# Softmax rows divided inside the transposing matmuls by a diagonal of reciprocals, and one adaLN chunk finished before the recurrence

## The chip, the cores and the metric

One core of one Trainium2 chip runs the whole step as a single program. The metric is the device time in microseconds (us) of one execution; less is better. The engines named below are PE (matmuls; its weight loads are listed as PEld), DVE (VectorE), ACT (ScalarE), POOL (GpSimd) and SP (SyncE, which issues most transfers).

## The reference, cut to what matters

One trunk layer over 1024 latent and 256 context tokens, model width 1024, in float32. The parts that the change touches are the attention and the adaLN modulation:

```python
def adaln(cond, w_ada, b_ada):
    m = jax.nn.silu(cond.astype(F32)) @ w_ada.astype(F32) + b_ada.astype(F32)
    return jnp.split(m[..., None, :], N_MOD, axis=-1)      # N_MOD = 6

def one_block(qi):                                          # per 128 queries
    s = jnp.einsum('bqkgd,bskd->bkgqs', qi, kf) * scale
    p = jax.nn.softmax(s, axis=-1)
    return jnp.einsum('bkgqs,bskd->bqkgd', p, vf)
```

There are 8 query heads of 64 channels over 2 key/value heads. Latent queries attend to 512 cached and 1024 latent keys; context queries attend to the 256 context keys. Beside the attention there is a gated linear recurrence (HGRN2, 4 heads, two directions), and after both come the output projections and a squared-ReLU MLP.

## The kernel before, in words

All matmuls of the projections and of the MLP are done as three float32r products of split operands (a high part `hi` and a low part `lo`, names `hs`, `wsp`, `ah`, `wh`), so PE is used three times for each weight tile (lines 319 to 321 and 336 to 338). Instructions on PE stand in the order in which the program is written; the other engines are ordered by a scheduler, which takes priorities (`tc.high_priority`) and explicit successions (`tc.issue_after`).

The attention is cut into units of one head and 256 queries (two blocks `j` of 128): 32 latent units with keys in three tiles of 512 (index `i`), and 8 context units with one tile of 256. For each block and key tile, `score` makes 128 x 512 scores (L819), DVE takes row maxima (L820), `expo` writes `pexp` on ACT with the row sums beside it (L830), DVE adds and inverts the sums into `rs` (L833, L834), and `norm` multiplies each tile of `pexp` in place by `rs` (L838), alternately on POOL and on DVE. Then `trans` transposes four 128 x 128 pieces of `pexp` into one PSUM tile `ps_t` by four PE instructions whose moving operand is the identity (L860); ACT and DVE split that tile into `pTh` and `pTl` (L863), and `value` multiplies the two by the values (L874, L875). A latent unit has six such steps, a context unit one, so there are 32 * 6 + 8 = 200 groups of four transposes. A list of events with fixed offsets orders these steps on PE, and between them a filler `fz` puts matmuls of other input projections and of the adaLN weights.

adaLN's weights come in 16 chunks of 256 columns. `ada_cols` multiplies a chunk (L176) into a PSUM tile of tag `g` (three buffers, shared with the projections' outputs), copies it out on ACT (`ev`, L178), and returns `late`, which transposes it into the same PSUM tile (L182), reduces it on DVE (`adas`, L185) and adds the bias (`modc`, L186). The `late` parts wait in the list `todo`, and are taken out during a later projection group.

After the attention, `hgrn` runs 24 recurrence units (head, direction, token tile), filled up with the gate projections. `prep` of a unit makes its decays and keys with scans and products on DVE, ACT and POOL (L1008 to L1044), `keys_t` transposes its keys `uf` on PE (L1072), `scores`, `states_` and `out` do the matmuls (L1083, L1095, L1114, L1116). `prep` of the next unit is placed behind the last copy of keys and the last product that made keys. The tile `R` that the scans read is set by POOL (L1244, L1245).

Of the kernel before, what the change touches and what calls it, by code (L numbers as in the profile page):

```python
# [12 lines left out]
ALU = mybir.AluOpType  # L13
AX = mybir.AxisListType

P = 128
# [28 lines left out]
def build(ctx, tc, I, O, C):  # L45
    nc = tc.nc
    v, s_, g_, pe, sp = nc.vector, nc.scalar, nc.gpsimd, nc.tensor, nc.sync
# [8 lines left out]
    def pool(name, side="left"):  # L56

        st = open_pools[name] = ExitStack()
        return st.enter_context(tc.tile_pool(name=name, bufs=1, side=side, reuse_waits="tile"))
# [13 lines left out]
    def PS(tag, shape=(P, 512)):  # L73
        tag = "g" if tag == "p" else tag
        return ps.tile(list(shape), F32, tag=tag, name="ps_" + tag, bufs=PSB[tag])

    def S(shape=(P, 512), dt=F32, name=None, ring=None):
        ring = ring or RING_OF[name]
        return (xb if ring == "X" else sb if ring in "DE" else sl).tile(list(shape), dt, tag="s" + ring, name=name, bufs=RINGS[ring])
# [14 lines left out]
    def T(n, name="tiny"):  # L94
        return tp.tile([P, n], F32, tag="tiny%d" % n, name=name, bufs=8 if n <= 16 else 2)
# [7 lines left out]
    def store(out, in_):  # L103
        g_.dma_start(out=f32(out), in_=f32(in_))

    def f32(ap):
        return ap.bitcast(F32)


    ident0 = S((P, P), name="ident0")  # L110
# [3 lines left out]
    ident = f32(ident_r)  # L114
# [53 lines left out]
    ones = cp.tile([P, 1], F32, name="ones")  # L168
    v.memset(ones, 1.0)

    def ada_cols(pa, raw, ci):

        for k in range(4):
            for q in range(4):
                kq = 4 * (q // 2) + k
                pe.matmul(pa[32 * q:32 * q + 32, 0:P], ada_l[:, kq, :], raw[:, kq, (q % 2) * P:(q % 2 + 1) * P], start=(k == 0), stop=(k == 3))  # L176
        ev = S((P, P), name="ev")
        s_.activation(ev, pa[:, 0:P], AF.Copy)  # L178

        def late():  # L180
            pt = pa[:, P:2 * P]
            pe.transpose(pt, ev, ident)  # L182
            x = T(4, "adas")
            with tc.high_priority(offset=600):
                v.tensor_reduce(x.rearrange("p (c r) -> p c r", c=2), pt.rearrange("p (i c x) -> p c x i", i=2, c=2)[:, :, 0:2, :], axis=AX.X, op=ALU.add)  # L185
            v.tensor_tensor(modc[:, :, ci:ci + 2], x.rearrange("p (c r) -> p r c", c=2),  # L186
                            cols[:, B_ADA + ci:B_ADA + ci + 2].unsqueeze(1).broadcast_to([P, 2, 2]), op=ALU.add)
        return late
# [240 lines left out]
    KG = [512, 512, 512, 256]  # L429
# [244 lines left out]
    for idx in range(len(steps)):  # L674
        if idx > KC:
            ahead(idx + AHEAD + (idx > 11) + (idx > 13))
        t, kc = steps[idx]
# [105 lines left out]
    class Unit:  # L783
# [24 lines left out]
        def score(self, j, i):  # L808
            nk = len(self.kts)
            if (j, i) == (0, 0):  # L810
                self.qh = q_at[self.h, self.t]
                self.ps, self.mx, self.sm, self.rs = {}, {}, {}, {}
            if i == 0:
                self.mx[j], self.sm[j] = T(4, "mx"), T(4, "sm")
            n = KG[self.kts[i]]
            q0 = self.q2 * 256 + j * P
            pq = PS("s")
            for var in range(2):
                pe.matmul(pq[:, 0:n], self.qh[:, q0:q0 + P], K[self.g][var][self.kts[i]], start=(var == 0), stop=(var == 1))  # L819
            v.tensor_reduce(self.mx[j][:, i:i + 1], pq[:, 0:n], axis=AX.X, op=ALU.max)  # L820
            self.ps[j, i] = pq
            if i == nk - 1:
                ngm = T(1, "ngm")
                v.tensor_reduce(ngm, self.mx[j][:, 0:nk], axis=AX.X, op=ALU.max, negate=True)  # L824
                self.mx[j] = ngm
# [7 lines left out]
                v.tensor_reduce(rs, self.sm[j][:, 0:nk], axis=AX.X, op=ALU.add)  # L833
                v.reciprocal(rs, rs)  # L834

        def norm(self, j, i):
            x = self.Ps[j][i][:, 0:KG[self.kts[i]]]
            NORM[(i + j) % len(NORM)].tensor_scalar(x, x, self.rs[j], None, op0=ALU.mult)  # L838

        def events(self, s0):  # L840
            if self.nstep == 1:
                ev = [(-4, 0, 0), (-3.5, 1, 0)]
                out = [(a, self.score, (j, i)) for a, j, i in ev]
                out += [(a + 1, self.expo, (j, i)) for a, j, i in ev]
                out += [(a + 2, self.norm, (j, i)) for a, j, i in ev]
            else:
                out = [(a, self.score, (j, i)) for (j, i), a in zip(self.tasks, (-7, -6.9, -6, -4, -3.9, -3))]
                out += [(a, self.expo, (j, i)) for (j, i), a in zip(self.tasks, (-5.4, -4.9, -4.4, -2.4, -1.9, -1.4))]
                out += [(a, self.norm, (j, i)) for (j, i), a in zip(self.tasks, (-4.35, -3.45, -2.45, -1.35, 0.1, 2.1))]
            for p2 in range(self.nstep):  # L850
                out.append((p2, self.trans, (p2,)))
                out.append((p2 + ((2.5, 2.3, 2.0, 1.7, 1.5, 1.3)[p2] if self.nstep > 1 else 1.5), self.value, (p2,)))
            return [(s0 + a, f, x) for a, f, x in out]

        def trans(self, p2):
            pt = PS("t", (P, 2, 256))
            for a in range(2):
                i, kg, b = self.kt[2 * p2 + a]
                for j in range(2):
                    pe.transpose(pt[:, a, j * P:(j + 1) * P], self.Ps[j][i][:, b * P:(b + 1) * P], ident)  # L860
            hi = S((P, 2, 256), F32R, name="pTh")
            lo = S((P, 2, 256), F32R, name="pTl")
            behind[:] = s_.activation(hi, pt, AF.Copy), v.tensor_tensor(lo, pt, f32(hi), op=ALU.subtract)  # L863
            self.pt[p2] = hi, lo
# [21 lines left out]
            if self.h % 2 == 1 and self.q2 == n // 256 - 1:  # L886
                dma(OA[self.h // 2][self.t], o_at[self.h // 2, self.t][:, 0:n])

    NORM = [g_, v]
    gone, keyed, copied = [None], [None], [None]  # L890
    q_at, o_at = {}, {}
    K = [[[None] * 4 for _ in range(2)] for _ in range(2)]
# [256 lines left out]
    def hgrn(fill, before):  # L1149

        units = [HUnit(6 * h + j, h, d, t) for h in range(4) for j, (d, t) in enumerate(((0, 0), (0, 1), (1, 1), (1, 0), (0, 2), (1, 2)))]
        fwd = {u.h: {} for u in units}
        for u in units:
            u.fwd = fwd[u.h].get(u.t)
            fwd[u.h][u.t] = u
        N, LATE = len(units), 3

        share = [u.n + 128.0 for u in units] + [300.0] * LATE
        tot, done, st = sum(share), 0.0, None
        with tc.issue_after(gone[0].ins):  # L1160
            units[0].prep()
        before()
        units[0].keys_t()
        for i in range(N + LATE):
            part = lambda x: fill.to((done + x * share[i]) / tot)
            if i + 1 < N:
                with ExitStack() as after:
                    after.enter_context(tc.issue_after(copied[0].ins))
                    after.enter_context(tc.issue_after(keyed[0].ins))
                    units[i + 1].prep()  # L1170
            if i < N:
                u = units[i]
                part(0.25)
                u.scores(u.fwd)
                part(0.5)
                u.states_(u.st or st)
                st = u.last
                if u.t == 2:
                    store(O["new_state_hgrn"][u.d, u.h], st)
                part(0.75)  # L1180
            if i >= LATE and units[i - LATE].d == 1:
                units[i - LATE].out_t()
            if 1 <= i <= N:
                units[i - 1].out(units[i - 1].fwd)
            part(0.95)
            if i + 1 < N:
                units[i + 1].keys_t()
            if 1 <= i <= N and units[i - 1].d == 1:
                units[i - 1].gate(units[i + 1] if i + 1 < N else None)
            part(1.0)  # L1190
            done += share[i]
# [17 lines left out]
    todo = []  # L1209
# [67 lines left out]
    for t in MT:  # L1277
        n = TT[t][1]
        for c in range(8):
            r = S(name="or")  # L1280
# [18 lines left out]
    for c2 in range(4):  # L1299
        r = wp.tile([P, 8, 256], F32, tag="wraw", name="wraw", bufs=2)  # L1300
        for i, nm in enumerate(("w_hgrn_out", "w_attn_out")):
            dma(r[:, 4 * i:4 * i + 4, :], I[nm][:, c2 * 256:(c2 + 1) * 256].rearrange("(k p) c -> p k c", p=P))
        for half in range(2):
# [4 lines left out]
            for t in MT:  # L1308
                n = TT[t][1]
# [108 lines left out]
    for b, half in turns:  # L1418
        t, off = b // 4, (b % 4) * P
# [62 lines left out]
    def raw1(i):  # L1482
        return wraw(I["w_ff1"], KC, i * 256)
# [30 lines left out]
    for i in range(NP):  # L1514
        r = raw1(i)
        for half in range(2):
            j = 2 * i + half
# [5 lines left out]
            if half == 0:  # L1523

                x = pw.tile([P, 4, P], F32, tag="at", name="at", bufs=4)
# [43 lines left out]
    ev = pool("ev", "right")  # L1569
    W2 = I["w_ff2"]  # L1570
    op0 = []
# [303 lines left out]
    x = fw_tile("y34")  # L1875
# [85 lines left out]
```

## Time and profile before

| | |
|---|---|
| time, median of 3 runs | 2056.77 us (2056.67 to 2057.38) |
| the profiled execution's own time | 2056.44 us |
| its span in the trace | 2054.7 us |
| granted TensorE clock, mean | 0.998 |
| PE busy | 2013.7 us (98%) |
| PE weight loads busy | 1735.2 us (84%) |
| DVE / ACT / POOL busy | 1407.0 / 941.1 / 533.1 us |

The span lies 1.7 us under the execution's time. "Busy" of PE is the union of its instructions' durations. A matmul's duration reaches past the start of the next one, so for PE the distance from start to start says what an instruction takes up; the timeline gives starts. A row of groups reads: line, engine, operation, output<-inputs, shapes, count, then busy time, mean duration of one, and the engine's idle time before them with what ended it. A row of the timeline reads: start, length, engine, line, operation, and in brackets the idle time before it; several like instructions are merged with their count.

### The profile page before, as it was taken

To read this page: it belongs to the slowest core of one execution; us is meant where nothing else is said; L and a number is where in the kernel's file an instruction comes from. 1 tells how busy PE (TensorE), PEld (TensorE's weight loads), DVE (VectorE), ACT (ScalarE), POOL (GpSimd) and SP (SyncE) were. 2 spreads that over 40 slices of the span, in tenths; PEclk is the share of its full clock that TensorE was granted. 3 is DMA by queue.
4 is the path that set the end of the run, shared out by engine and by line. 5 is a ranking of instruction groups with operands and counts; after the bars stand their busy time and mean duration, and the time that the engine had idled before them with its cause. 6 is when DMAs were issued, how large, how long until landed. Compare 5 with 4: busy or idle time off the path is not lost.

```text
span 2054.7 us, 33792 instructions
## 1 busy us (share of the span) xinstructions
PE 2013.7 (98%) x12470; PEld 1735.2 (84%) x12470; DVE 1407.0 (68%) x2733; ACT 941.1 (46%) x1973; POOL 533.1 (26%) x526
## 2 busy tenths in 40 slices
PE   7899999999999999999999999999999999999998
PEld 5698889988889978888888889988888888888886
DVE  5866776767776788879254635886666666577686
ACT  4634555555555423333321335755455544333443
POOL 1452233333333355545112101222122110000120
PEclk9999999999999999999999999999999999999999
DMA  9452220321212454554644533854444489455764
GB/s 318 160 189 78 70 83 32 104 88 55 77 50 80 132 176 158 165 168 158 199 136 149 179 113 119 253 184 152 159 146 157 145 292 361 147 160 175 232 238 142
DMA packets 220612, 317.38 MB, mean 154 GB/s; under 512 B 18760, under 2 KB 139808, under 8 KB 220448
## 3 DMA queue, kind: packets, MB, share of 16 engines
q1 hardware_dynamic: 207968, 275.32, 41.8%
q0 software_dynamic: 12480, 39.91, 5.2%
q8 instruction: 98, 1.61, 0.3%
q14 instruction: 66, 0.54, 0.1%
HBM read 229.43 MB, written 85.74 MB: 153 GB/s over the span
## 4 chain that ended last, share of the span: by engine, by line
PE 87%; DVE 6%; DMA 3%; ACT 2%; issue 1%; SPq 0%; POOL 0%; POOLq 0%; DVEq 0%; ACTq 0%
PE ps_g L319 8%; PE ps_g L321 7%; PE ps_g L320 7%; PE ps_s L819 4%; PE ps_t L860 4%; PE ps_g L1749 2%; PE ps_g L1748 2%; PE ps_g L1750 2%; PE ps_s L1593 2%; PE ps_s L1594 2%; PE ps_s L1595 2%; PE ps_g L875 2%; PE ps_s L1748 2%; PE ps_s L1749 2%; PE ps_s L1750 2%; PE ps_g L336 2%
## 5 line engine op out<-in xcount | busy, mean ns | idle before, releaser
L319 PE MATMUL ps_g<-hs,wsp 128*128 128x512 f32 (+1 forms) x896 | 322.5, 360 | 4.0 <-DVE adas L185 4.0
L321 PE MATMUL ps_g<-hs,wsp 128*128 128x512 f32 (+1 forms) x896 | 309.6, 345 | 0.0
L320 PE MATMUL ps_g<-hs,wsp 128*128 128x512 f32 (+1 forms) x896 | 309.3, 345 | 0.0
L838 POOL TENSOR_SCALAR pexp<-pexp,rs 128x512 f32<-128x512 f32 (+1 forms) x104 | 169.4, 1635 | 367.0 <-ACT pTh L863 174.4
L286 ACT ACTIVATE wsp<-wraw 128x512 fp32r<-128x512 f32 (+1 forms) x186 | 116.7, 667 | 228.6 <-PE ps_g L320 90.8
L287 DVE TENSOR_TENSOR wsp<-wraw,wsp 128x512 fp32r<-128x512 f32 (+1 forms) x186 | 147.0, 812 | 98.2 <-ACT wsp L286 97.7
L319 PEld LDWEIGHTS ps_g<-hs,wsp 128*128 128x128 f32 x896 | 169.9, 190 | 24.9 <-issue 4.6
L321 PEld LDWEIGHTS ps_g<-hs,wsp 128*128 128x128 f32 x896 | 169.5, 189 | 21.6
L863 ACT ACTIVATE pTh<-ps_t 128x512 fp32r<-128x512 f32 x200 | 118.6, 603 | 143.8 <-PE ps_t L860 142.4
L320 PEld LDWEIGHTS ps_g<-hs,wsp 128*128 128x128 f32 x896 | 170.2, 190 | 15.0
L286 ACT ACTIVATE ah<-ar 128x640 fp32r<-128x640 f32 (+1 forms) x112 | 80.9, 723 | 186.5 <-PE ps_g L1749 102.3
L820 DVE TENSOR_REDUCE mx<-ps_s 128x1 f32<-128x512 f32 (+1 forms) x208 | 137.2, 663 | 41.6 <-PE ps_s L819 40.7
L830 ACT ACTIVATE pexp<-ps_s,ngm 128x512 f32<-128x512 f32 (+1 forms) x208 | 137.5, 670 | 36.0 <-DVE ngm L824 35.2
L863 DVE TENSOR_TENSOR pTl<-ps_t,pTh 128x512 fp32r<-128x512 f32 x200 | 135.4, 680 | 18.0 <-ACT pTh L863 17.8
L287 DVE TENSOR_TENSOR ah<-ar,ah 128x640 fp32r<-128x640 f32 (+1 forms) x112 | 91.9, 821 | 77.0 <-ACT ah L286 75.8
L819 PE MATMUL ps_s<-Kl,Ql 128*128 128x512 f32 (+1 forms) x416 | 131.0, 412 | 1.0 <-ACT pexp L830 0.9
L860 PE MATMUL ps_t<-ident,pexp 128*128 128x128 f32 x800 | 121.4, 273 | 4.3 <-DVE pexp L838 3.0
L336 PE MATMUL ps_g<-wsp,hs 128*128 128x256 f32 x400 | 115.9, 290 | 0.0
L338 PE MATMUL ps_g<-wsp,hs 128*128 128x256 f32 x400 | 112.9, 282 | 0.0
L337 PE MATMUL ps_g<-wsp,hs 128*128 128x256 f32 x400 | 112.6, 281 | 0.0
L875 PE MATMUL ps_g<-pTl,Vl 128*128 128x256 f32 x400 | 105.4, 286 | 3.6 <-DVE pTl L863 3.5
L860 PEld LDWEIGHTS ps_t<-ident,pexp 128*128 128x128 f32 x800 | 93.7, 140 | 16.2 <-DVE pexp L838 4.6
(422 smaller groups left out, 5379.1 us busy)
## 6 DMA issues: line engine op xcount, KB each, us to landing
ar<-AF SPq DMA_DIRECT2D x112, 320.0 KB, 3.3
wraw<-in_w_ff SPq DMA_DIRECT2D x32, 1024.0 KB, 6.2
wr<-in_w_ff SPq DMA_DIRECT2D x128, 256.0 KB, 4.3
wraw<-in_w_in SPq DMA_DIRECT2D x18, 1024.0 KB, 5.6
wraw<-in_w_ada SPq DMA_DIRECT2D x16, 1024.0 KB, 5.7
AF<-a POOLq DMA_DIRECT2D x48, 256.0 KB, 2.8
AF<-t POOLq DMA_DIRECT2D x48, 256.0 KB, 2.3
wa<-in_w_ada SPq DMA_DIRECT2D x32, 256.0 KB, 6.0
```

Source lines behind the costliest of these rows:

```text
L286: s_.activation(hi, raw, AF.Copy)
L287: return v.tensor_tensor(lo, raw, f32(hi), op=ALU.subtract)
L319: pe.matmul(out, hi[:, k, :], mh, start=(first and k == 0), stop=False)
L320: pe.matmul(out, hi[:, k, :], ml, start=False, stop=False)
L321: pe.matmul(out, lo[:, k, :], mh, start=False, stop=(last and k == kcs - 1))
L336: pe.matmul(po[:, bb, :], mh[:, off:off + P], wh[:, k % 4, :], start=(k == 0), stop=False)
L819: pe.matmul(pq[:, 0:n], self.qh[:, q0:q0 + P], K[self.g][var][self.kts[i]], start=(var == 0), stop=(var == 1))
L830: s_.activation(e[:, 0:n], self.ps.pop((j, i))[:, 0:n], AF.Exp, bias=self.mx[j], accum_out=self.sm[j][:, i:i + 1])
L838: NORM[(i + j) % len(NORM)].tensor_scalar(x, x, self.rs[j], None, op0=ALU.mult)
L860: pe.transpose(pt[:, a, j * P:(j + 1) * P], self.Ps[j][i][:, b * P:(b + 1) * P], ident)
L863: behind[:] = s_.activation(hi, pt, AF.Copy), v.tensor_tensor(lo, pt, f32(hi), op=ALU.subtract)
L875: pe.matmul(pv[:, 0:256], V[self.g][kg][:, b, :], lo[:, a, :], start=False, stop=(k == last))
```

## The change

Three things are edited.

1. `norm` and its 208 instructions go. In their place `diag` writes, once for each block of 128 queries, the identity scaled by `rs` into one of four slots of a new tile `dg` (80 DVE instructions of 128 x 128). `trans` multiplies `pexp` (stationary) by that slot (moving) with an ordinary matmul, in the place of the transposes against the identity.
2. `dg` lies in the same one-buffer ring `K` as `ident0` before it and `R` after it.
3. The last chunk's `late` part is called ahead of the recurrence's loop, behind the first unit's `keys_t`, and the second unit's `prep` is placed behind that chunk's reduction `adas`.

```diff
@@ ada_cols.late
-                v.tensor_reduce(x..., pt..., axis=AX.X, op=ALU.add)
+                adas[0] = v.tensor_reduce(x..., pt..., axis=AX.X, op=ALU.add)
@@ Unit
-        def norm(self, j, i):
-            x = self.Ps[j][i][:, 0:KG[self.kts[i]]]
-            NORM[(i + j) % len(NORM)].tensor_scalar(x, x, self.rs[j], None, op0=ALU.mult)
+        def diag(self, j):
+
+            DG["n"] += 1
+            self.dg[j] = DG["t"][:, DG["n"] % 4]
+            v.tensor_scalar(self.dg[j], ident, self.rs[j], None, op0=ALU.mult)
...
-                out += [(a, self.norm, (j, i)) for (j, i), a in zip(self.tasks, (-4.35, -3.45, -2.45, -1.35, 0.1, 2.1))]
+                out += [(a, self.diag, (j,)) for j, a in ((0, -4.35), (1, -1.35))]
...
-                    pe.transpose(pt[:, a, j * P:(j + 1) * P], self.Ps[j][i][:, b * P:(b + 1) * P], ident)
+                    pe.matmul(pt[:, a, j * P:(j + 1) * P], self.Ps[j][i][:, b * P:(b + 1) * P], self.dg[j], start=True, stop=True)
...
-    NORM = [g_, v]
+    DG = {"n": 0, "t": S((P, 4, P), name="dg")}
@@ hgrn
         units[0].keys_t()
+        todo.pop()()
         for i in range(N + LATE):
...
+                    if i == 0:
+                        after.enter_context(tc.issue_after(adas[0].ins))
                     after.enter_context(tc.issue_after(copied[0].ins))
```

The lines of the kernel behind the edits move down by two to seven: L860 becomes L864, L176 becomes L178, L1072 becomes L1076, L1008 becomes L1012.

On PE in the attention, one latent step before, from its transposes to the next step's values:

```order
L860 MATMUL ps_t<-ident,pexp 128x128 x4
L819 MATMUL ps_s<-Kl,Ql 128x512 x2
L336 MATMUL ps_g<-wsp,hs 128x256
L337 MATMUL ps_g<-wsp,hs 128x256
L338 MATMUL ps_g<-wsp,hs 128x256
```

And now, on the same engine at the same place:

```order
L864 MATMUL ps_t<-dg,pexp 128x128 x4
L821 MATMUL ps_s<-Kl,Ql 128x512 x2
L338 MATMUL ps_g<-wsp,hs 128x256
L339 MATMUL ps_g<-wsp,hs 128x256
L340 MATMUL ps_g<-wsp,hs 128x256
```

Nothing moved there; the four instructions have another moving operand and are no longer marked as transposes.

On DVE in the same stage, around one block's reciprocal, before (`oa` is a unit's output, `ze` a projection's):

```order
L884 TENSOR_TENSOR oa<-ps_g,pvt 64x256
L833 TENSOR_REDUCE rs<-sm 128x1
L834 RECIPROCAL rs<-rs 128x1
L838 TENSOR_SCALAR pexp<-pexp,rs 128x512
L863 TENSOR_TENSOR pTl<-ps_t,pTh 128x512
L820 TENSOR_REDUCE mx<-ps_s 128x1
```

And now:

```order
L888 TENSOR_TENSOR oa<-ps_g,pvt 64x256
L835 TENSOR_REDUCE rs<-sm 128x1
L836 RECIPROCAL rs<-rs 128x1
L842 TENSOR_SCALAR dg<-ident,rs 128x128
L867 TENSOR_TENSOR pTl<-ps_t,pTh 128x512
L822 TENSOR_REDUCE mx<-ps_s 128x1
```

The diagonal stands directly behind the reciprocal, where one of the two engines' products stood; the later products of the same block are gone.

On DVE at the start of the recurrence, before, around the second unit's first scan (the first `L1034` row is the first unit's keys):

```order
L1034 TENSOR_TENSOR uf<-usf,um 128x512
L980 SCALAR_TENSOR_TENSOR ze<-ze,ps_g 128x512
L1008 SCALAR_TENSOR_TENSOR ucp<-R,uf 128x512
L1009 SCALAR_TENSOR_TENSOR usf<-uf,R 128x511
L1010 MEMSET usf 128x1
```

and 27 rows further down, where the last chunk's reduction stood:

```order
L287 TENSOR_TENSOR wsp<-wraw,wsp 128x512 x2
L1028 TENSOR_TENSOR um<-um,ucp 128x4
L1044 TENSOR_TENSOR um<-um,ucp 128x4
L185 TENSOR_REDUCE adas<-ps_g 128x4
L1104 SCALAR_TENSOR_TENSOR ust<-s_9203,udec,ps_s 128x128
```

Now:

```order
L1038 TENSOR_TENSOR uf<-usf,um 128x512
L984 SCALAR_TENSOR_TENSOR ze<-ze,ps_g 128x512
L289 TENSOR_TENSOR wsp<-wraw,wsp 128x512 x2
L984 SCALAR_TENSOR_TENSOR ze<-ze,ps_g 128x512
L187 TENSOR_REDUCE adas<-ps_g 128x4
L1012 SCALAR_TENSOR_TENSOR ucp<-R,uf 128x512
L1013 SCALAR_TENSOR_TENSOR usf<-uf,R 128x511
```

The reduction now stands ahead of the second unit's scans instead of behind all of its work and the third unit's scans, and with it two splits of weights and one product of `ze` came ahead of those scans.

On PE at that place, before (the `x16` row is the chunk's product; its transpose `L182` stood 30 rows behind this `L1072`, just ahead of the first `L1095`):

```order
L338 MATMUL ps_g<-wsp,hs 128x256
L176 MATMUL ps_g<-wraw,ada_l 32x128 x16
L1072 MATMUL ps_t<-ident,uf 128x128 x4
L319 MATMUL ps_g<-hs,wsp 128x512
L320 MATMUL ps_g<-hs,wsp 128x512
```

Now:

```order
L340 MATMUL ps_g<-wsp,hs 128x256
L178 MATMUL ps_g<-wraw,ada_l 32x128 x16
L1076 MATMUL ps_t<-ident,uf 128x128 x4
L184 MATMUL ps_g<-ident,ev 128x128
L321 MATMUL ps_g<-hs,wsp 128x512
```

The chunk's transpose follows its product at a distance of four instructions.

More of the change, by code (lines that the diff above doesn't have):

```diff
@@ L169, in build @@
     v.memset(ones, 1.0)
+    adas = [None]
     def ada_cols(pa, raw, ci):
@@ L184, in late @@
             with tc.high_priority(offset=600):
-                v.tensor_reduce(x.rearrange("p (c r) -> p c r", c=2), pt.rearrange("p (i c x) -> p c x i", i=2, c=2)[:, :, 0:2, :], axis=AX.X, op=ALU.add)
+                adas[0] = v.tensor_reduce(x.rearrange("p (c r) -> p c r", c=2), pt.rearrange("p (i c x) -> p c x i", i=2, c=2)[:, :, 0:2, :], axis=AX.X, op=ALU.add)
             v.tensor_tensor(modc[:, :, ci:ci + 2], x.rearrange("p (c r) -> p r c", c=2),
@@ L811, in score @@
                 self.qh = q_at[self.h, self.t]
-                self.ps, self.mx, self.sm, self.rs = {}, {}, {}, {}
+                self.ps, self.mx, self.sm, self.rs, self.dg = {}, {}, {}, {}, {}
             if i == 0:
@@ L844, in events @@
                 out += [(a + 1, self.expo, (j, i)) for a, j, i in ev]
-                out += [(a + 2, self.norm, (j, i)) for a, j, i in ev]
+                out += [(a + 2, self.diag, (j,)) for a, j, i in ev]
             else:
```

2 rows, old and new, of the table RING_OF are left out of this document.

## The prediction

> **What bounds the kernel now.** I read the page's engine rows first, then the costliest groups, the waits of PE, and the timeline where the change sits.
>
> ```profile
> PE 2013.7 (98%) x12470; PEld 1735.2 (84%) x12470; DVE 1407.0 (68%) x2733; ACT 941.1 (46%) x1973; POOL 533.1 (26%) x526
> ...
> PE 87%; DVE 6%; DMA 3%; ACT 2%; issue 1%; SPq 0%; POOL 0%; POOLq 0%; DVEq 0%; ACTq 0%
> ...
> L838 POOL TENSOR_SCALAR pexp<-pexp,rs 128x512 f32<-128x512 f32 (+1 forms) x104 | 169.4, 1635 | 367.0 <-ACT pTh L863 174.4
> ...
> L860 PE MATMUL ps_t<-ident,pexp 128*128 128x128 f32 x800 | 121.4, 273 | 4.3 <-DVE pexp L838 3.0
> ```
>
> PE is busy for 98% of the span and is 87% of the chain that ended last. The 104 products on POOL look dear (169.4 us) but POOL is busy 26%. The page's 4.3 us is all that PE ever idled ahead of the 800 transposes. So the question is what each edit takes from PE or adds to it. By stage, and with PE's waits in the attention:
>
> ```profile
> 160.00:260.00 100.00, 97.33 (x647) 83.60 (x646) 71.78 (x156) 56.07 (x136) 33.01 (x20) 1.00 0.23 76
> ...
> 460.00:560.00 100.00, 99.00 (x670) 86.43 (x670) 72.27 (x156) 57.31 (x139) 33.64 (x20) 1.00 0.21 68
> ```
> ```profile
> PE ps_g L875 <- DVE pTl L863: 3.5, 6, 1.0
> PE ps_t L860 <- DVE pexp L838: 3.0, 6, 1.1
> PE ps_t L860 <- DVE pTl L863: 1.1, 2, 0.9
> PE ps_s L819 <- ACT pexp L830: 0.9, 3, 0.5
> ```
>
> The first two rows are stretches of 100 us (length, then busy time of PE, PEld, DVE, ACT, POOL): PE 97 to 99, DVE 72, ACT 57. The waits, in total, times and longest, for 160 to 710 us, sum to 8.5 us in 17 places. Nothing but PE bounds this stage.
>
> **The diagonal product in the place of the transpose.** This is the term that decides. The new instruction is an ordinary float32 matmul of 128 x 128 by 128 columns, and the recurrence has both kinds with these shapes:
>
> ```profile
> L1095 PE MATMUL ps_s<-uv,ukt 128*128 128x128 f32 x160 | 22.0, 276 | 0.0
> L1072 PE MATMUL ps_t<-ident,uf 128*128 128x128 f32 x80 | 12.7, 273 | 0.0
> ```
>
> Each unit of the recurrence issues as many L1095 as L1072 (one per block; 80 in the program), but the trace has 160 of the first and 80 of the second. A float32 product is carried out as two weight loads and two matmuls, a transpose as one. What that takes up is read from start to start; the first three rows are a group of four products, then four transposes, then four transposes in the attention:
>
> ```profile
> 726.30 1.06 PE L1095 MATMUL ps_s<-uv,ukt 128*128 128x128 f32 x8
> 727.12 0.48 PE L319 MATMUL ps_g<-hs,wsp 128*128 128x512 f32 x1
> 727.43 0.40 PE L320 MATMUL ps_g<-hs,wsp 128*128 128x512 f32 x1
> ...
> 731.30 0.60 PE L1072 MATMUL ps_t<-ident,uf 128*128 128x128 f32 x4
> 731.65 0.48 PE L319 MATMUL ps_g<-hs,wsp 128*128 128x512 f32 x1
> 731.97 0.39 PE L320 MATMUL ps_g<-hs,wsp 128*128 128x512 f32 x1
> ```
> ```profile
> 409.87 0.60 PE L860 MATMUL ps_t<-ident,pexp 128*128 128x128 f32 x4
> 410.22 0.36 PE L336 MATMUL ps_g<-wsp,hs 128*128 128x256 f32 x1
> 410.42 0.28 PE L337 MATMUL ps_g<-wsp,hs 128*128 128x256 f32 x1
> ```
>
> From the first of four products to the second matmul behind them are 727.43 - 726.30 = 1.13 us; for four transposes with the same follower 731.97 - 731.30 = 0.67 us. The difference is 0.46 us a group. From the merged lengths the same follows: eight reach 1.06, four 0.60, so one more costs 0.46 / 4 = 0.115 us. In the attention four transposes and their follower take 410.42 - 409.87 = 0.55 us with a shorter follower, so the group itself costs there what it costs in the recurrence. The steps have two decimals; I take 0.455 us, between 0.448 (four at 0.112, if the roundings fall low) and 0.46. Over 32 * 6 + 8 = 200 groups that is 91 us, from 89.6 to 92. PE stands in order and is never more than some per cent idle in this stage, so nothing beside it hides this: the whole term lies on the path.
>
> The Trainium skill ("TensorE: Matmul & The Clock Gate", section Terms) says that the transpose mode is four times faster for FP32, and "FP8 and Floating Point Precision" (TensorE Precision Notes) gives true FP32 four passes. By that rule a group would become 4 instead of 2.05 times as long; the trace shows two records per product and half that price, and the measurement decides, but the rule is kept as a rival.
>
> **The products that go, and the diagonal that comes.** 208 products leave POOL and DVE; 80 writes of 128 x 128 come to DVE.
>
> ```profile
> L838 DVE TENSOR_SCALAR pexp<-pexp,rs 128x512 f32<-128x512 f32 x96 | 58.1, 632 | 1.5
> ...
> L1104 DVE SCALAR_TENSOR_TENSOR ust<-ust,udec,ps_s 128x128 f32<-128x128 f32 x64 | 21.9, 343 | 5.2 <-PE ps_s L1095 4.0
> ```
>
> The diagonal's price isn't in the trace: above nothing, under the 0.63 us of a product on a tile four times as large; the nearest row in shape is 0.34 us. Taken at 0.34, 80 cost 27 us of DVE against 58 that go, so DVE falls and its cost to PE is nothing; even at 0.63 it is 50 against 58. The chain to the first transposes becomes shorter (one write instead of a POOL product of 1.6 us), and each step of PE 0.46 us longer, while ACT and DVE have the same splits to do. So the waits above should nearly all go: 8.5 us, and a wait costs more than its idle time, since it also cuts the overlap of the previous instruction (0.27 long, one each 0.11): at most 17 * 0.16 = 2.7 us more. I take 9 of these 11.2 us. If the cover were gone, at worst the four rows stay: 0 recovered.
>
> `R` now waits for the last product that reads `dg`, as its buffer is the same:
>
> ```profile
> 702.54 0.49 PE L860 MATMUL ps_t<-ident,pexp 128*128 128x128 f32 x3
> ...
> 708.84 1.70 DVE L1008 TENSOR_TENSOR_SCAN ucp<-R,uf 128x512 f32<-128x512 f32 x1
> ...
> L1244 POOL MEMSET R<- x1: 525/525/525, 6.9 to 6.9; 128x512 f32 x1
> ```
>
> From about 703.0 us POOL needs 0.65 us (a second, small set is 0.13 us), and the first scan starts 5.8 us later: hidden. Should POOL be held up, the first scan comes late by what exceeds 5 us.
>
> **The chunk ahead of the recurrence.** Here lies the only long stall of PE behind the first stages:
>
> ```profile
> 717.65 1.57 DVE L1008 TENSOR_TENSOR_SCAN ucp<-R,uf 128x512 f32<-128x512 f32 x1
> ...
> 726.20 0.27 PE L182 MATMUL ps_g<-ident,ev 128*128 128x128 f32 x1
> ...
> 733.58 0.39 PE L321 MATMUL ps_g<-hs,wsp 128*128 128x512 f32 x1
> 737.92 0.39 PE L319 MATMUL ps_g<-hs,wsp 128*128 128x256 f32 x1 [3.96 <-DVE adas L185]
> ```
> ```profile
> 737.00:739.00 2.00, 1.07 (x10) 0.94 (x14) 2.00 (x6) 0.00 (x0) 1.94 (x2) 0.94 0.94 352
> 739.00:741.00 2.00, 2.00 (x33) 1.50 (x30) 1.97 (x7) 0.00 (x0) 0.00 (x0) 0.50 0.04 16
> 741.00:743.00 2.00, 2.00 (x14) 2.00 (x14) 2.00 (x3) 0.00 (x0) 1.66 (x1) 0.71 0.22 65
> ```
>
> The transpose is done at 726.2, but the reduction that frees its PSUM buffer stands on DVE behind two preps and runs at 737.7; PE wants a third buffer at 733.8. From start to start 4.34 us pass instead of 0.23: 4.1 us. Behind it the granted clock (the column ahead of the DMA share) is 0.94, 0.50 and 0.71 in three stretches of 2 us, a loss of 2 * (0.06 + 0.50 + 0.29) = 1.7 us of PE. The Trainium skill ("TensorE: Matmul & The Clock Gate", What's actually happening) has the array at half clock after an idle window of some 3.4 us until a busy one; the trace agrees (3.96 us idle, then 0.50). With the reduction early, both go: 5.8 us.
>
> The move costs on PE a wait of the transpose for the copy `ev`:
>
> ```profile
> 719.67 0.66 PE L1072 MATMUL ps_t<-ident,uf 128*128 128x128 f32 x4
> ...
> 719.85 0.28 ACT L178 ACTIVATE ev<-ps_g 128x128 f32<-128x128 f32 x1 [0.44 <-PE ps_g L176]
> ```
>
> The four transposes are through at 720.1, the copy at 720.13: between 0 and 0.5 us with the signal's way, taken as 0.3. On DVE the new wait holds the second unit's whole prep: its scan starts behind the reduction, about 720.9 instead of 717.65. Behind it are POOL's products of that unit, and PE's L1072 at 731.30. But two splits and one product that stood between (about 2 us) come ahead of it, and that prep has slack of its own:
>
> ```profile
> 729.44 0.69 DVE L1034 TENSOR_TENSOR uf<-usf,um 128x512 f32<-128x512 f32 x1 [2.65 <-POOL usf L1025]
> ```
>
> DVE idles 2.65 us before the keys while POOL waits its turn. 3.25 us of delay against about 2 and 2.65: I take nothing, and 4 us if it isn't covered. No DMA is moved but the first loads of that prep, which SP issues in the same order.
>
> **The sum**, against the profiled execution's 2056.44 us: + 91 - 9 - 5.8 + 0.3 = 2132.9 us. The median of the runs is 0.33 us above that execution: 2133.3 us.
>
> **Rivals.** *A product costs PE what a transpose did.* For it: the shapes are equal and the page's mean durations too (276 and 273 ns). Against it: the doubled count of L1095. Then only the waits go: 2056.8 - 9 - 5.5 = 2042.3 us, faster; it decides as soon as the surcharge of a group is under 14.5 / 200 = 0.07 us. Chance 0.04. *The product takes four times a transpose*: a group of four transposes takes 4 * 0.11 = 0.44, three more 1.32 us, times 200 is 264; 2056.8 + 264 - 14.5 = 2306 us. Against it: 1.13 against 0.67 us above. This is the time of the skill's rule. Chance 0.02. *The late second prep gives the stall back*: PE waits at L1076 or at the scores for keys that start 3.25 us later, so 4 us stay and perhaps the half clock with them: 2137 to 2139 us. For it: DVE is busy without a gap from 730 to 745 us. Against it: the slack shown. Chance 0.12. *The surcharge vanishes in idle time*: PE's idle time in the whole stage is under 11 us, so it can't.
>
> **How the numbers follow.** 0.82 for the forecast, 0.12, 0.04 and 0.02 for the rivals. Low end: 89.6 and all waits gone, 2056.8 + 89.6 - 11.2 - 5.8 = 2129; high end: 92 and nothing recovered, 2149, where the likelier part of it, the third rival with half the attention's waits kept, is 2144. The range is 2127 to 2145, which leaves out the two other rivals and the far end. 0.2% (4 us) is about what a measurement can tell from no change; all but the first rival are slower by far more: slower 0.95, same 0.01, faster 0.04.
>
> **What would show it.** In the profile after, L864 should have 1600 records on PE and as many weight loads, with PE busy about 2100 us; eight in a row should reach 1.06 us; no wait of 4 us before a projection's matmul behind `adas`, and no half clock there; POOL down by about 169 us; the four waits near 1 us in all. 800 records, or a pitch other than 0.11 us, would make the main term wrong; a wait of PE at L1076 or L1087 of the second unit, the small one.

## The result: 72 us slower

The changed kernel takes 2128.77 us (median of 4 runs, 2128.29 to 2129.66) against 2056.76 us: a ratio of 1.0347, 95% interval 1.0335 to 1.0360. The profiled execution is the slowest of its four, 2129.66 us with a span of 2127.5. The page of the kernel after, engine rows, chain and the costliest groups that answer to those shown before:

```profile
PE 2097.4 (99%) x13270; PEld 1830.6 (86%) x13270; DVE 1380.2 (65%) x2709; ACT 946.3 (44%) x1973; POOL 364.3 (17%) x422
...
PE 97%; DVE 1%; ACT 1%; DMA 1%; issue 0%; SPq 0%; POOL 0%; POOLq 0%; DVEq 0%; ACTq 0%
...
L864 PE MATMUL ps_t<-dg,pexp 128*128 128x128 f32 x1600 | 211.2, 275 | 0.3 <-DVE dg L842 0.3
```

800 transposes became 1600 records on PE, and PE now holds 97% of the chain. POOL lost 168.8 us of work; what that was worth is tried below. One group in the attention's timeline, with the matmul behind it:

```profile
401.67 1.05 PE L864 MATMUL ps_t<-dg,pexp 128*128 128x128 f32 x8
402.48 0.71 PE L821 MATMUL ps_s<-Kl,Ql 128*128 128x512 f32 x2
```

It holds PE for 402.48 - 401.67 = 0.81 us. The four transposes quoted in the prediction held it for 410.22 - 409.87 = 0.35 us. The difference is 0.46 us, 200 times. Below is the attention as one stretch, from its first transpose to its last, before and after (window, length, then busy time of PE, PEld, DVE, ACT, POOL):

```profile
169.20:702.80 533.60, 525.24 (x3807) 475.05 (x3805) 381.99 (x861) 304.02 (x730) 175.04 (x109) 1.00 0.23 75
```
```profile
169.40:779.20 609.80, 609.54 (x4605) 569.56 (x4604) 352.16 (x837) 308.37 (x730) 9.01 (x7) 1.00 0.20 66
```

The stage grew by 76.2 us, and PE's idle time in it fell from 8.4 to 0.3 us. From the first `L1072` to the last `L1144` the recurrence shrank from 285.2 to 280.4 us. What lies outside the two differs by up to 3 us between the traces below, whatever the edit. So 76.2 - 4.8 = 71.4 of the 72 us lie in the two places of the change.

### The profile page after: what moved, and what is told of

It reads as the page before. It is cut to its first block, busy times and chain, and to the rows that moved or that the text cites. A ratio compares the mean times of both kernels' runs of the same rounds, so it can differ in the third digit from the quotient of the medians.

```text
span 2127.5 us, 35033 instructions
## 1 busy us (share of the span) xinstructions
PE 2097.4 (99%) x13270; PEld 1830.6 (86%) x13270; DVE 1380.2 (65%) x2709; ACT 946.3 (44%) x1973; POOL 364.3 (17%) x422
## 4 chain that ended last, share of the span: by engine, by line
PE 97%; DVE 1%; ACT 1%; DMA 1%; issue 0%; SPq 0%; POOL 0%; POOLq 0%; DVEq 0%; ACTq 0%
PE ps_t L864 8%; PE ps_g L321 8%; PE ps_g L323 8%; PE ps_g L322 8%; PE ps_s L821 4%; PE ps_g L1757 2%; PE ps_g L1756 2%; PE ps_g L1755 2%; PE ps_g L338 2%; PE ps_g L879 2%; PE ps_g L878 2%; PE ps_g L340 2%; PE ps_g L339 2%; PE ps_s L1600 2%; PE ps_s L1602 2%; PE ps_s L1601 2%
## 5 line engine op out<-in xcount | busy, mean ns | idle before, releaser
L864 PE MATMUL ps_t<-dg,pexp 128*128 128x128 f32 x1600 | 211.2, 275 | 0.3 <-DVE dg L842 0.3
L864 PEld LDWEIGHTS ps_t<-dg,pexp 128*128 128x128 f32 x1600 | 199.6, 191 | 6.8 <-issue 0.8
L986 POOL TENSOR_TENSOR ze<-ze,hnb 128x512 f32<-128x512 f32 x10 | 14.2, 1425 | 633.0 <-DVE ze L984 326.8
L878 PE MATMUL ps_g<-pTh,Vl 128*128 128x256 f32 x400 | 103.8, 282 | 0.0
```

What stands on the lines that cost most here:

```text
L864: pe.matmul(pt[:, a, j * P:(j + 1) * P], self.Ps[j][i][:, b * P:(b + 1) * P], self.dg[j], start=True, stop=True)
L878: pe.matmul(pv[:, 0:256], V[self.g][kg][:, b, :], hi[:, a, :], start=(k == 0), stop=False)
```

## The experiments

Times are medians; ratios are to runs of the kernel before that were made beside them on the same chip (its medians there were 2056.5 and 2057.1 us).

**The chunk alone** (`chunk_only`):

```diff
         units[0].keys_t()
+        todo.pop()()
...
+                    if i == 0:
+                        after.enter_context(tc.issue_after(adas[0].ins))
```

> The kernel before with the third edit alone (the last chunk's late part ahead of the recurrence). If the edits add up, this one is worth the 4.8 us by which the recurrence got shorter between the two traces: 2056.8 - 4.8 = 2052.0 us, with no wait of 4 us behind adas and no half clock. Rival: the second unit's late prep takes it back, or the gain came from the lighter DVE queue of the other edit: 2056 to 2057 us.

2051.81 us, ratio 0.9978 (0.9968 to 0.9988). The recurrence takes 280.3 us, and no wait of PE behind `adas` is left. The 4.7 us are as the edits' sum would have them. The rival that a late second unit takes the gain back falls, and so does the one of the lighter DVE queue; a new wait of PE of 0.7 us on the third unit's products is left, and is read further down.

**The diagonal alone** (`diag_only`), the changed kernel without those lines:

> The changed kernel without the third edit. If the edits add up: 2128.8 + 4.8 = 2133.6 us, with the 4 us wait behind adas back. Rival (the lighter queues alone shorten that wait): 2129 to 2131 us.

2135.49 us, ratio 1.0381 (1.0367 to 1.0395): 6.7 us over the changed kernel, 1.9 more than told. Its timeline, and stretches of 2 us behind it:

```profile
814.64 0.58 PE L321 MATMUL ps_g<-hs,wsp 128*128 128x256 f32 x1 [4.05 <-DVE adas L187]
```
```profile
813.00:815.00 2.00, 0.35 (x1) 0.36 (x2) 2.00 (x6) 0.00 (x0) 2.00 (x2) 0.58 1.05 382
815.00:817.00 2.00, 2.00 (x22) 1.73 (x25) 1.99 (x6) 0.00 (x0) 0.65 (x1) 0.50 0.27 101
817.00:819.00 2.00, 2.00 (x28) 1.57 (x21) 1.97 (x3) 0.00 (x0) 0.94 (x1) 0.50 0.00 0
819.00:821.00 2.00, 2.00 (x14) 2.00 (x14) 2.00 (x4) 0.00 (x0) 1.10 (x2) 0.71 0.64 188
```

The stall is back at its old length (4.05 us), and the granted clock (0.58, 0.50, 0.50, 0.71) is low for about twice as long as in the kernel before (0.94, 0.50, 0.71). Not all of that is lost: PE still stands until 814.64, and for the 0.35 us that it works in the first stretch I take half clock. The loss is then 0.35 * 0.50 + 2 * (0.50 + 0.50 + 0.29) = 2.8 us, against 1.7 in the kernel before. The recurrence takes 286.0 us, 0.8 more than there and 5.6 more than in the changed kernel, and the attention takes 609.8 us in both. So the longer half clock explains about 0.8 of the 1.9 us that the sum missed; where the rest lies isn't settled.

**No division at all** (`no_division`): the changed kernel with transposes, and no diagonals.

```diff
-                out += [(a, self.diag, (j,)) for j, a in ((0, -4.35), (1, -1.35))]
...
-                    pe.matmul(pt..., self.Ps[j][i]..., self.dg[j], start=True, stop=True)
+                    pe.transpose(pt..., self.Ps[j][i]..., ident)
```

> The changed kernel with the transposes against the identity put back and no division by the row sums anywhere (the softmax rows stay undivided): no surcharge on PE, no products on POOL and DVE, the chunk early. Surcharge of 91 us: 2128.8 - 91 = 2038 us, if the waits in the attention (14.7 us by start to start) went because the products went. Rival: they went because PE became slower; then most of them are back here, 2046 to 2052 us. Rival on the main term, a product costs what a transpose costs: 2128 us.

2041.01 us, ratio 0.9926 (0.9913 to 0.9938): 87.8 us under the changed kernel, between the first expectation and its rival and nearer to the first. The attention's stretch:

```profile
169.80:691.50 521.70, 520.40 (x3807) 475.38 (x3805) 329.30 (x758) 304.04 (x730) 9.02 (x7) 1.00 0.24 76
```

With the same PE program as before in this stage it is 11.9 us shorter: what the 208 products cost there, and so the most that any scheme that only takes them off POOL and DVE can win in it. Against the kernel after it is 88.1 us shorter, where the surcharge is 91; the rest of 3 us fits waits that a faster PE still runs into: PE idles 1.3 us in this stretch against 0.3.

**The product without the diagonal** (`product_and_norm`): the divisions stay, only the transposes become products with the identity.

```diff
-                    pe.transpose(pt..., self.Ps[j][i]..., ident)
+                    pe.matmul(pt..., self.Ps[j][i]..., ident, start=True, stop=True)
```

> The kernel before with nothing changed but the transposes, which become ordinary float32 products with the identity; the 208 divisions stay on POOL and DVE and the chunk stays late. Surcharge 91 us: 2147.8 us if the waits in the attention stay, as they belong to the divisions; 2056.8 + 91 - 14.7 = 2133 us if the slower PE alone hides them. Rival on the main term, equal cost: 2057 us.

2134.25 us, ratio 1.0377 (1.0363 to 1.0391), equal to `diag_only` within the intervals. All of PE's waits in its attention, and the stretch:

```profile
PE ps_t L860 <- DVE pexp L838: 0.5, 1, 0.5
```
```profile
171.20:781.70 610.50, 610.04 (x4606) 569.55 (x4605) 390.10 (x861) 308.63 (x730) 175.57 (x109) 1.00 0.20 66
```

POOL and DVE do all their divisions here (175.6 and 390.1 us), and the stage is nearly as long as without them (610.5 against 609.8). So the waits went because PE became slower, and taking the divisions away added at most 0.7 us to that. My first theory, that they went with the products, falls for the changed kernel, though `no_division` shows that it would hold if PE had stayed as it was.

**Half of the products** (`half_products`): as the last one, with two of every four.

```diff
+                    if a == 0:
+                        pe.matmul(pt..., self.Ps[j][i]..., ident, start=True, stop=True)
+                    else:
                         pe.transpose(pt..., self.Ps[j][i]..., ident)
```

> The kernel before with two of every four transposes as ordinary float32 products with the identity; divisions stay, the chunk stays late. Price of a product by count: 400 * 0.114 = 45.6 us more of PE. If the waits of the attention are hidden in proportion to how much slower PE becomes: 2056.8 + 45.6 - 7 = 2095 us. If half of the slowing already hides all of them: 2056.8 + 45.6 - 13.6 = 2089 us. Rival (the price is one for the change of mode in a group, not one for each product): 2148 or 2057 us.

2093.70 us, ratio 1.0172 (1.0158 to 1.0185): between the two expectations, and its interval, 2089.6 to 2095.2, comes close to both. The price goes with the number of products, since 2148 and 2057 us are far off. The stage tells more than the time. From its first transpose to its last pass 568.0 us, 34.4 more than before and 11.2 less than the 45.6 by count: three quarters of the waits are hidden by half of the slowing. Its waits in the attention:

```profile
PE ps_g L878 <- DVE pTl L866: 0.7, 2, 0.5
PE ps_t L861 <- DVE pexp L838: 0.5, 1, 0.5
PE ps_t L861 <- DVE pTl L866: 0.3, 1, 0.3
```

**The product in float32r** (`product_f32r`):

```diff
-            e = self.Ps[j][i] = S(name="pexp")
+            e = self.Ps[j][i] = S(dt=F32R, name="pexp")
...
-    DG = {"n": 0, "t": S((P, 4, P), name="dg")}
+    DG = {"n": 0, "t": S((P, 4, P), F32R, name="dg")}
```

> The changed kernel with the softmax rows and the diagonal held as float32r, so that the transposing product is a float32r one; the rows lose the low part of each value by that. If it is the float32 type that makes a product two loads and two matmuls, the trace has 800 records at L864 and PE loses the surcharge: as without any division, 2041 us. Rival, it is the missing transpose mode: 1600 records and 2128 us.

2046.58 us, ratio 0.9944 (0.9931 to 0.9958). Its weight loads and matmuls of that line:

```profile
L864 PE MATMUL ps_t<-dg,pexp 128*128 128x128 f32 x800 | 113.9, 264 | 2.2 <-DVE dg L842 1.3 <-DVE pTl L867 0.7
L864 PEld LDWEIGHTS ps_t<-dg,pexp 128*128 128x128 f32 x800 | 110.1, 190 | 10.8 <-issue 3.2 <-DVE dg L842 2.3
```

800 records instead of 1600: an ordinary product is doubled by its float32 type, and leaving the transpose mode doesn't double it by itself. The time misses the 2041 us told by 5.6: the attention takes 527.2 us instead of 521.7. With 512-column followers, the median from the start of a group to the second matmul behind it is 0.68 us here and 0.67 in `no_division`, some 2 us over 200 groups, and with PE fast again it waits for the diagonals (1.3 us on the list). Where the rest of the 5.5 us lies isn't settled. This version keeps only the high part of each softmax value, so it stands for the price and not as a replacement.

**The division at the output** (`divide_late`), with the chunk early:

```diff
                 self.pv = PS("p")
+                for j in range(2):
+                    pe.transpose(self.pv[:, 256 + j * P:256 + (j + 1) * P], self.rs[j].broadcast_to([P, P]), ident)
...
-            gone[0] = v.tensor_tensor(oa, pv[d0:d0 + 64, 0:256], tm..., op=ALU.add)
+            v.tensor_tensor(oa, pv[d0:d0 + 64, 0:256], tm..., op=ALU.add)
+            gone[0] = v.tensor_tensor(oa, oa, pv[d0:d0 + 64, 256:512], op=ALU.mult)
```

> A version meant to beat both: the chunk early, transposes against the identity, rows left undivided, and the division made on the output of the unit: the reciprocals are transposed as a broadcast into the free half of the output's PSUM bank (two transposes a unit, 80 in all) and DVE multiplies the 64 x 256 output by them (40 products). PE: 2041 us as without division + 80 * 0.11 = 8.8 us, so 2050 us, about the same as with the chunk alone (2051.8). Rival, the waits for the last product of a unit or for the reciprocals come on top: 2055 us or more. Other rival, the transposes of the reciprocals fill waits: 2042 to 2045 us.

2051.45 us, ratio 0.9966 (0.9953 to 0.9978): faster than before and after, as forecast, and not to be told from the chunk alone (0.9968 to 0.9988). Its attention takes 529.2 us, between 521.7 and 533.6: the 80 transposes of reciprocals and the products at the output took back 7.5 of the 11.9 us that the divisions had cost there.

## Why the prediction was right, step by step

The time came out 4.5 us under the 2133.3 us forecast, inside the range. That it lies inside is partly luck: the low end that the prediction worked out is 2129.4 us (all waits gone), the time fell 0.6 us below it, and the range holds it only because it starts at 2127, 2 us lower, for which no reason is given.

- **The surcharge** (91 us taken) was right, and for the reason given: the doubled records of `L1095` against `L1072` are a property of a float32 product, as `product_f32r` and `half_products` show. The groups of the attention bear the size out: where two matmuls of 512 columns follow, the median from the group's start to the second of them is 0.670 us before and 1.126 after, so 0.456 us a group, and 91 us for 200. The rivals of equal and of fourfold price fall: PE's group takes 0.81 against 0.35 us. The rule of the Trainium skill on the transpose mode ("TensorE: Matmul & The Clock Gate", Terms: four times faster for FP32) is not borne out by these runs; at these 128 columns the factor is 2.3 in this reading, or 1600 records against 800.
- **The waits of the attention** are the term that was mis-sized. The step took 9 us and called 11.2 us the most; the stage gave 91 - 76.2 = 14.8 us. A count that doesn't use the 91 us agrees: what the stage's steps from start to start take beyond the median step of their kind (where it is over 0.03 us) adds up to 26.1 us before and 12.3 after, a difference of 13.8. The cap was built from the list of waits (8.5 us) plus 0.16 us for each of its 17 entries. But the list shows only waits that outlast the modelled end of the instruction before, so shorter ones have no entry at all. Summed from the starts in the trace, the steps from `L874` to `L875` lost 5.4 us where the list had 3.5: 4.5 in its six entries, which the 0.16 us each allow for, and the rest in steps without an entry. Of the two reasons that the step gave, the longer steps of PE were enough alone; the shorter chain was not needed.
- **The diagonals and `R`** were hidden as told:

```profile
L842 DVE TENSOR_SCALAR dg<-ident,rs 128x128 f32<-128x128 f32 x80 | 23.5, 299 | 6.6 <-PE ps_t L864 4.4
```
```profile
779.57 0.53 POOL L1251 MEMSET R<- 128x512 f32 x1 [2.06 <-PE ps_t L864]
780.16 0.13 POOL L1252 MEMSET R<- 128x16 f32 x1
```
```profile
785.32 1.71 DVE L1012 TENSOR_TENSOR_SCAN ucp<-R,uf 128x512 f32<-128x512 f32 x1
```

  A diagonal takes 0.30 us (0.34 taken), and DVE fell by 29.8 us in the stage (31 by the step's numbers). POOL waits 2.06 us for the last product, and `R` is ready 5.0 us ahead of the first scan.
- **The chunk** was taken at 5.5 us net and gave 4.7 alone and 4.8 in the trace. The new wait on DVE came and was covered, as forecast:

```profile
797.46 0.15 DVE L187 TENSOR_REDUCE adas<-ps_g 128x4 f32<-128x8 f32 x1
797.53 1.21 DVE L1012 TENSOR_TENSOR_SCAN ucp<-R,uf 128x512 f32<-128x512 f32 x1
...
806.30 0.68 DVE L1038 TENSOR_TENSOR uf<-usf,um 128x512 f32<-128x512 f32 x1
```
```profile
796.15 0.66 PE L1076 MATMUL ps_t<-ident,uf 128*128 128x128 f32 x4
796.67 0.33 PE L184 MATMUL ps_g<-ident,ev 128*128 128x128 f32 x1
...
807.87 0.60 PE L1076 MATMUL ps_t<-ident,uf 128*128 128x128 f32 x4
```

  Counted from the first unit's key transposes, the second unit's scan starts 797.53 - 796.15 = 1.4 us behind them, where it had stood 2.0 us ahead: 3.4 us late. Its keys start 10.15 us behind them against 9.77 before, so the slack took 3 us of it, and they are done 0.9 us before PE wants them. The copy `ev` cost little: from the key transposes to the projection behind them pass 0.60 us, against 0.41 before without the chunk's transpose, which took 0.10 in its old place (726.20 to 726.30), so about 0.1 us is left for the wait where 0.3 was taken. Counted from the first unit's key transposes, PE reaches the second unit's `L1099` 5.6 us sooner than before, but the third unit's only 4.7 us sooner. The rest is lost just there:

```profile
827.29 1.10 DVE L1108 SCALAR_TENSOR_TENSOR ust<-ust,udec,ps_s 128x128 f32<-128x128 f32 x3
```
```profile
827.32 0.39 PE L323 MATMUL ps_g<-hs,wsp 128*128 128x512 f32 x1
828.49 1.13 PE L1099 MATMUL ps_s<-uv,ukt 128*128 128x128 f32 x8 [0.79 <-issue]
```

  From start to start 1.17 us pass instead of 0.23, about 0.95 us lost. `L1099` writes a buffer of tag `s`, which has three; in the order of the program it is the one that held the second unit's products, and `ust` on DVE is their reader. The profile names no releaser, but the last `ust` ends 0.10 us ahead of the first product here, and so it does in all four other runs with the chunk early, where the listed wait is 0.7 to 0.9 us; no run with the chunk late has it. Before, that `ust` ended 31.4 us behind the first key transposes and PE came at 37.0; now it ends at 32.2, and PE would have come at 31.4. So the third rival came true for a sixth of the gain, though not at the two places that the prediction told to watch.
- **The sum** with the measured terms: 2056.8 + 91 - 14.8 - 4.8 = 2128.2 us, against 2128.8. As the 14.8 is itself what the stage leaves of the 91, this shows only that the two places hold nearly all of the change.

## What to carry to other kernels

Before an identity is replaced by a scaled diagonal in a transpose, count the records of an ordinary product of the same type in the trace: "free" scaling on the bound engine cost 91 us here to take away work that, with its waits, was worth 12. A list of waits is a lower bound of what a slower or lighter neighbour can give back; the length of the stage between two marks is the measure. And two remedies for the same wait do not add: each of them alone removed most of the 14.8 us (11.9 without the divisions, 91 - 76.9 = 14.1 with the slower PE).

## What the runs showed of the hardware that was not expected

The same stall of 4 us on PE was followed by 3.4 us of half clock in the kernel before and by 6.8 us in `diag_only`, `product_and_norm` and `half_products`. In the first the clock fell 0.8 us after PE had gone on (738.75 against 737.92); in the other three it fell 0.7 to 1.3 us before PE went on. Their recurrences are 0.7 to 1.0 us longer than the first one's, so that is how much the price of one stall varied between executions. That the place of the fall sets the length isn't shown by four cases.

A float32r product of 128 columns took one weight load and one matmul, with a median of 0.111 us from start to start, against 0.109 for a float32 transpose, while a float32 product took two of each at 0.112. The mean durations (264, 273 and 275 ns) tell nothing of that price. Float32r products step by 0.12 us at 256 columns and by 0.23 at 512, so at 128 columns the step isn't set by the number of columns. How much more a float32 product costs than a transpose at more columns no run here shows.
